# A decoder layer with a state-space branch: the order of the state-space batches' parts

## The chip, the cores and the metric

The kernel runs on one core of one Trainium2 chip. The metric is device time in microseconds (us) of one execution, as the median of several. The engines are TensorE (PE in the profile; its weight loads are PEld), VectorE (DVE), ScalarE (ACT), GpSimd (POOL) and SyncE (SP, which here only issues DMAs). Each engine takes its instructions from its own queue in a fixed order.

## The reference

One layer over 1024 tokens of width 1024, all in float32:

```
proj = rms_norm(h, pre_norm_g) @ w_in
u_ssm, z_ssm, q, k, v, z_attn = split(proj)
# state-space branch: 32 groups of 16 channels, each with a 64-wide complex state
bu = einsum('blgp,gnp->blgn', u, b_bar)
states = associative_scan(s[t] = lam_bar * s[t-1] + bu[t])
y = einsum('blgn,gpn->blgp', states, c).real + d * u
g = gelu(y)
ssm_out = g * sigmoid(g @ w_glu + b_glu) * silu(z_ssm)
# attention branch: window of 128 tokens, ALiBi, a sink logit per head
attn_out = swa(q, k, v, sinks) * silu(z_attn)
mixed = concat(ssm_out, attn_out) @ w_out
h = h + rms_norm(mixed, post_norm_g)
h = h + sigmoid(h @ pl_w_gate + pl_b_gate) * (p @ pl_w_proj)
```

## The kernel before

**Matrix products.** A projection is computed to full precision as three products of rounded parts, hi*hi, hi*lo and lo*hi (`products`, L115 to L126). Weights come in from DRAM to `w_st` (L98), ScalarE rounds them to `w_hi` (L92), and VectorE makes the rest `w_lo` (L93). A projection of 128 output columns over all tokens is 48 matmuls of 128x512.

**The state-space branch** is cut into eight batches of four groups. 1024 steps are cut into 128 chunks of 8. Within a chunk the recurrence is written as matrices, over the chunks a scan of 128 steps runs. For each batch:

- `into_states` (L513) loads the inputs `U` and the coefficients `coef` by SyncE; makes the matrix `mt` by three VectorE products (L335, the helper `tt`); transposes it on TensorE (L536) and copies it to `m` on ScalarE (L537); multiplies `U` by `m` (L541) and copies the result `w` (L543); makes the copy `w2` of `w` with its two halves of partitions exchanged, by two DMAs issued from ScalarE (L591, L592); makes the short-range matrix `t7` (L547, VectorE), writes it to DRAM four times (L558) and reads it back as the Toeplitz matrix `tz` (L560); and makes the output matrix `qt` by three VectorE products.
- `phases` (L568) makes `co` and `si`, the turning factors, by six VectorE products.
- `scan` (L595) turns `w` by `w2*si`, `w*co` and their sum, runs the scan on VectorE (L602) into `s`, and makes the exchanged copy `s2` by two DMAs from SyncE.
- `outputs` (L607) turns `s` back (`s2*si`, `s*co`, their difference), multiplies by `tz` and `qt` on TensorE (L615, L617), applies gelu on ScalarE (L619) into `y`, and stores `y` to DRAM (L622).

Most of these tiles come from pools of one or two buffers each, shared by a tag: `w` and `s` share the tag "w"; `w2`, `s2` and `y` the tag "sw"; the temporary products the tag "ta"; all three tags have two buffers. A tile that is asked for later takes the buffer of the tile asked for two before it, when that one's last reader is done.

**Order.** The program is written once, in order, and a planner lays out every engine's queue from it: each instruction's place is its place in the text, blocks under `high_priority(offset=20)` count as 20 instructions earlier, and the planner takes what by its own reckoning of times is ready first. What it has laid out is fixed when the kernel runs. `issue_after(x)` puts the instructions of its block behind instruction x on x's engine.

The main loop (L693) runs, for each batch c, at high priority: `scan(c)`, `phases(c+1)`, `outputs(c)`, `into_states(c+1)`. Then come one or two of eleven projections (v, four of q, four of z_attn, two of z_ssm).

**What follows the batches.** The last two z_ssm projections (`SsmGate`, L843) need nothing of the state space. The gate products of the state-space branch (`Glu`, L880; matmuls L903) read `y_all`, the outputs of all eight batches reloaded from DRAM by eight DMAs (L923), which SyncE issues behind the last exchange of `s`. The attention units (`Unit`, L744: scores L764 and L765, transposes L803, values L821) run beside the gate products and the first half of the output projection; their ScalarE parts are issued behind the gelu of the last batch (L983). Their queries are split to `bq_hi` and `bq_lo` (L733) in buffers that the state-space batches used before (tags "mt", "tz", "m" and "sw"). Then come the rest of the output projection, the norm, and the last gate product.

Of the kernel before, what the change touches and what calls it, by code (L numbers as in the profile page):

```python
# [20 lines left out]
P = 128  # L21
# [32 lines left out]
def layer_kernel(  # L54
# [6 lines left out]
    with ExitStack() as top:  # L61
# [272 lines left out]
        def tt(o, a, b, op):  # L334
            V.tensor_tensor(out=o, in0=a, in1=b, op=op)  # L335
# [144 lines left out]
        def big(name, tag):  # L480
            return t2([P, WID], F32, name, tag)
# [16 lines left out]
        def of_in(L, c):  # L498
            return L[:, c * GB : c * GB + GB, :].unsqueeze(2).broadcast_to([P, GB, PC, CH])
# [4 lines left out]
        def view_in(t):  # L504
            return t.rearrange("p (g q k) -> p g q k", k=CH, q=PC)

        def view_out(t):
            return t.rearrange("p (g k q) -> p g k q", k=CH, q=PC)
# [1 line left out]
        def ev(t):  # L510
            return t.rearrange("p (g a b) -> p g a b", a=8, b=16)

        def into_states(b):  # L513

            c = b["c"]
            gs = slice(c * GB, (c + 1) * GB)
            U = b["U"] = t2([P, GB, NC], F32, "U", "u")
            nc.sync.dma_start(out=U, in_=u_dr[c // 2][(c % 2) * 64 : (c % 2) * 64 + 64].rearrange("(g q) j c -> (q j) g c", q=PC))
            coef = b["coef"] = t2([P, GB, 4, PC], F32, "coef", "coef")
            with tc.issue_after(loaded.ins):  # L520
                nc.sync.dma_start(out=coef, in_=bc[:, gs])

            t1, mt = big("t1", "ta"), big("mt", "mt")
            def per_in(n):
                return coef[:, :, n, :].unsqueeze(3).broadcast_to([P, GB, PC, CH])

            def per_out(n):
                return coef[:, :, n, :].unsqueeze(2).broadcast_to([P, GB, CH, PC])

            tt(view_in(t1), of_in(LB_re_, c), per_in(0), ALU.mult)  # L530
            tt(view_in(mt), of_in(LB_im_, c), per_in(1), ALU.mult)
            tt(mt, t1, mt, ALU.subtract)
            m = big("m", "m")
            ps = bank("tab")
            for g in range(GB):
                PE.transpose(ps[:, g * P : (g + 1) * P], mt[:, g * P : (g + 1) * P], ident)  # L536
            S.copy(out=m, in_=ps)  # L537
            w = b["w"] = big("w", "w")
            ps = bank("w")
            for g in range(GB):  # L540
                PE.matmul(ps[:, g * NC : (g + 1) * NC], lhsT=m[:, g * P : (g + 1) * P], rhs=U[:, g, :],  # L541
                          start=True, stop=True)
            S.copy(out=w, in_=ps)  # L543
            b["w2"] = swapped(w, nc.scalar)
            ps = bank("tab")
            for g in range(GB):
                PE.matmul(ps[:, g * PC : (g + 1) * PC], lhsT=mt[:, g * P : (g + 1) * P],  # L547
                          rhs=coef[:, g, 2, :], start=True, stop=True)
            t7 = b["t7"] = t2([P, GB, PC], F32, "t7", "t7")
            tt(t7, last.unsqueeze(1).broadcast_to([P, GB, PC]),  # L550
               ddt[:, gs].unsqueeze(2).broadcast_to([P, GB, PC]), ALU.mult)
            tt(t7, t7, ps[:, 0 : GB * PC].rearrange("p (g q) -> p g q", q=PC), ALU.add)


            n, o = 2 * CH * PC, t7_dr[c].offset
            tz = b["tz"] = big("tz", "tz")
            for g in range(GB):
                nc.sync.dma_start(out=bass.AP(tensor=t7_dr.tensor, offset=o + g * PC * n + n - PC, ap=[[n, PC], [-PC, CH], [1, PC]]), in_=t7[:, g, :])  # L558
            for g in range(GB):
                nc.sync.dma_start(out=tz[:, g * P : (g + 1) * P],  # L560
                                  in_=bass.AP(tensor=t7_dr.tensor, offset=o + g * PC * n + CH * PC, ap=[[n, PC], [-PC, CH], [1, P]]))
            a, qt = big("t2", "ta"), big("qt", "qt")
            tt(view_out(a), of_out(L_re, c), per_out(2), ALU.mult)
            tt(view_out(qt), of_out(L_im, c), per_out(3), ALU.mult)
            tt(qt, a, qt, ALU.add)
            b["qt"] = qt

        def phases(b):  # L568
            gs = slice(b["c"] * GB, (b["c"] + 1) * GB)
            co, si = b["co"], b["si"] = big("co", "co"), big("si", "si")  # L570

            def a_(t):
                return t[:, gs, :].unsqueeze(3).broadcast_to([P, GB, 8, 16])

            def b_(t):
                return t[:, gs, :].unsqueeze(2).broadcast_to([P, GB, 8, 16])

            a = big("t3", "ta")
            tt(ev(a), a_(e1[1]), b_(e0[1]), ALU.mult)
            tt(ev(co), a_(e1[0]), b_(e0[0]), ALU.mult)  # L580
            tt(co, co, a, ALU.subtract)
            a = big("t4", "ta")
            tt(ev(a), a_(e1[0]), b_(e0[1]), ALU.mult)
            tt(ev(si), a_(e1[1]), b_(e0[0]), ALU.mult)
            tt(si, si, a, ALU.add)

        swaps = []

# [5 lines left out]

        def scan(b):  # L595
            w, w2, co, si, c = (b[n] for n in ("w", "w2", "co", "si", "c"))
            tt(w2, w2, si, ALU.mult)
            tt(w, w, co, ALU.mult)
            tt(w, w, w2, ALU.add)
            s = b["s"] = big("s", "w")  # L600
            for g in range(GB):
                V.tensor_tensor_scan(out=s[:, g * NC : (g + 1) * NC],  # L602
                                     data0=r8[:, c * GB + g : c * GB + g + 1].broadcast_to([P, NC]),
                                     data1=w[:, g * NC : (g + 1) * NC], initial=0.0, op0=ALU.mult, op1=ALU.add)
            b["s2"] = swapped(s, nc.sync)

        def outputs(b):  # L607
            s, s2, co, si, c, U, tz, qt = (b[n] for n in ("s", "s2", "co", "si", "c", "U", "tz", "qt"))
            tt(s2, s2, si, ALU.mult)
            tt(s, s, co, ALU.mult)  # L610
            tt(s, s, s2, ALU.subtract)
            y = t2([P, GB, NC], F32, "y", "sw")
            ps = bank("y")
# [71 lines left out]
        batch = [dict(c=c) for c in range(G // GB)]  # L685
        k_copies = [partial(copy_k, kv, part) for kv in range(2) for part in (kk_hi, kk_lo)]
        with tc.high_priority(offset=AHEAD):
            into_states(batch[0])
            phases(batch[0])
        project_k()  # L690
# [1 line left out]
                 + [partial(project_z_ssm, m) for m in range(2)])  # L692
        for c, b in enumerate(batch):  # L693
            with tc.high_priority(offset=AHEAD):
                scan(b)
                if c + 1 < len(batch):
                    phases(batch[c + 1])
                outputs(b)
                if c + 1 < len(batch):
                    into_states(batch[c + 1])  # L700
            for f in tiles[len(tiles) * c // len(batch) : len(tiles) * (c + 1) // len(batch)]:
                f()
                if k_copies and c > 1:
                    with tc.issue_after(w_last[0].ins):
                        k_copies.pop()()
# [479 lines left out]
```

## Time and profile before

| | us |
|---|---|
| median of 3 runs | 532.2 |
| lowest and highest of them | 531.94, 533.16 |
| the profiled execution | 531.67 |
| its span, from the first to the last instruction | 529.9 |
| the first scan of a batch begins | 90.0 |
| the last scan of a batch ends | 235.85 |

The profile is of one execution. Its rows give for a group of instructions the line of the kernel, the engine, the operation, the output tile and the input tiles, the shapes, and how many there were. In a row of the timeline the first number is the start and the second the duration, both in us from the start of the span; a row with x4 spans four instructions; the bracket at its end tells how long the engine was idle ahead of it, and on what it waited. Matmuls overlap, so the distance from one start to the next says more than a matmul's duration. ACTq and SPq rows are the issuing of DMAs. "Granted clock" is the share of full speed that TensorE's clock had.

### The profile page before, as it was taken

Reading aid. Unit: us, or ns where it says so; the run is one execution under the profiler, and the core shown is the slowest. Engines: PE = TensorE matmul, PEld = TensorE weight load, DVE = VectorE, ACT = ScalarE, POOL = GpSimd, SP = SyncE. Lnnn points to the kernel's source line nnn. Section 1 sums busy time; section 2 is a strip of 40 time slices with the busy share of each in tenths; the row PEclk is TensorE's granted clock in tenths of the full one; section 3 lists DMA queues with packets and bytes.
Section 4 is the critical chain, followed back from the end, with each engine's and each line's share of the span. In section 5 each row is a group of like instructions: output and inputs, shape, how many; then the busy total and the mean of one; then the engine's idle time right before and its main releaser. Section 6 shows DMA issues by size and latency. Waiting matters only on the chain.

```text
span 529.9 us, 7312 instructions
## 1 busy us (share of the span) xinstructions
PE 516.9 (98%) x2477; PEld 409.0 (77%) x2477; DVE 374.6 (71%) x865; ACT 211.7 (40%) x442; POOL 27.5 (5%) x69
## 2 busy tenths in 40 slices
PE   7999999999999999997899999999999999999996
PEld 6888888888888888884355766777788788888886
DVE  4879999879789979654878566555756659846232
ACT  5875121311222222124655655566734343333221
POOL 1000000000000000204020211100000000000000
PEclk9999999999999999999799999999999999999999
DMA  7972633445343344547755222101112155125112
GB/s 265 375 239 61 232 86 98 126 109 156 106 127 103 95 137 114 168 140 216 244 176 169 81 71 49 51 21 41 61 58 80 43 176 154 46 81 177 61 40 79
DMA packets 47092, 65.04 MB, mean 123 GB/s; under 512 B 10064, under 2 KB 25936, under 8 KB 47056
## 3 DMA queue, kind: packets, MB, share of 16 engines
q1 hardware_dynamic: 43664, 58.09, 34.5%
q0 software_dynamic: 1536, 4.20, 3.3%
q10 hardware_dynamic: 1856, 2.31, 1.7%
q8 instruction: 19, 0.31, 0.3%
q14 instruction: 17, 0.14, 0.1%
HBM read 44.12 MB, written 11.01 MB: 104 GB/s over the span
## 4 chain that ended last, share of the span: by engine, by line
PE 51%; DMA 2%; DVE 1%; SPq 0%; issue 0%; ACT 0%; ACTq 0%
PE ps_mm L126 9%; PE ps_mm L124 9%; PE ps_mm L122 9%; PE ps_mm L903 5%; PE ps_tab L122 3%; PE ps_tab L124 3%; PE ps_tab L126 3%; PE ps_w L821 2%; PE ps_y L821 2%; PE ps_tab L764 1%; PE ps_tab L765 1%; DMA y_all<-y_dr 1%; PE ps_w L803 1%; PE ps_y L803 1%; DMA y_dr<-y 1%
## 5 line engine op out<-in xcount | busy, mean ns | idle before, releaser
L122 PE MATMUL ps_mm<-x_hi,w_hi 128*128 128x512 f32 x272 | 86.2, 394 | 1.1 <-ACT x_hi L190 1.1
L126 PE MATMUL ps_mm<-x_hi,w_lo 128*128 128x512 f32 x272 | 86.9, 394 | 0.0
L124 PE MATMUL ps_mm<-x_lo,w_hi 128*128 128x512 f32 x272 | 85.7, 393 | 0.7 <-DVE x_lo L191 0.6
L92 ACT ACTIVATE w_hi<-w_st 128x512 fp32r<-128x512 f32 (+1 forms) x63 | 39.1, 621 | 100.9 <-PE ps_mm L124 68.9
L122 PEld LDWEIGHTS ps_mm<-x_hi,w_hi 128*128 128x128 f32 x272 | 50.9, 189 | 11.5 <-ACT x_hi L190 1.5
L124 PEld LDWEIGHTS ps_mm<-x_lo,w_hi 128*128 128x128 f32 x272 | 50.7, 188 | 11.6 <-DVE x_lo L191 1.5
L93 DVE TENSOR_TENSOR w_lo<-w_st,w_hi 128x512 fp32r<-128x512 f32 (+1 forms) x63 | 42.3, 671 | 24.3 <-ACT w_hi L92 24.3
L126 PEld LDWEIGHTS ps_mm<-x_hi,w_lo 128*128 128x128 f32 x272 | 50.7, 188 | 10.0
L903 PE MATMUL ps_mm<-y_all,w_glu 128*128 128x512 f32 x64 | 31.4, 637 | 3.5 <-DMA y_all<-y_dr 3.4
L122 PE MATMUL ps_mm<-h_hi,w_hi 128*128 128x512 f32 (+1 forms) x96 | 30.8, 380 | 0.0
L124 PE MATMUL ps_mm<-h_lo,w_hi 128*128 128x512 f32 (+1 forms) x96 | 30.8, 380 | 0.0
L126 PE MATMUL ps_mm<-h_hi,w_lo 128*128 128x512 f32 (+1 forms) x96 | 30.7, 380 | 0.0
L788 ACT ACTIVATE sc<-sc,mx 128x129 f32<-128x129 f32 x64 | 25.1, 395 | 12.7 <-DVE mx L781 12.5
L903 PEld LDWEIGHTS ps_mm<-y_all,w_glu 128*128 128x128 f32 x64 | 12.3, 203 | 17.7 <-issue 12.5
L1082 DVE SCALAR_TENSOR_TENSOR o_t<-o_t,pls 128x512 f32<-128x512 f32 (+1 forms) x17 | 10.8, 657 | 19.7 <-ACT o_t L1081 19.7
L335 DVE TENSOR_TENSOR sw<-sw,si 128x512 f32<-128x512 f32 x16 | 11.0, 686 | 16.5 <-DMA sw<-s 9.0
L122 PE MATMUL ps_mm<-m_hi,w_hi 128*128 128x512 f32 x64 | 22.1, 405 | 0.0
L126 PE MATMUL ps_mm<-m_hi,w_lo 128*128 128x512 f32 x64 | 21.8, 398 | 0.0
L124 PE MATMUL ps_mm<-m_lo,w_hi 128*128 128x512 f32 x64 | 21.7, 403 | 0.0
L122 PEld LDWEIGHTS ps_mm<-h_hi,w_hi 128*128 128x128 f32 x96 | 18.0, 188 | 3.5
L124 PEld LDWEIGHTS ps_mm<-h_lo,w_hi 128*128 128x128 f32 x96 | 18.1, 188 | 3.5
L126 PEld LDWEIGHTS ps_mm<-h_hi,w_lo 128*128 128x128 f32 x96 | 18.0, 188 | 3.4
(281 smaller groups left out, 1036.7 us busy)
## 6 DMA issues: line engine op xcount, KB each, us to landing
w_st<-in_w_in SPq DMA_DIRECT2D x30, 256.0 KB
w_st<-in_w_out SPq DMA_DIRECT2D x16, 256.0 KB
w_st<-in_w_gate SPq DMA_DIRECT2D x16, 256.0 KB
x<-in_xS SPq DMA_DIRECT2D x8, 512.0 KB
out_T<-o_t SPq DMA_DIRECT2D x15, 256.0 KB
x_sq<-in_xT SPq DMA_DIRECT2D x4, 512.0 KB
x_st<-in_x SPq DMA_DIRECT2D x4, 512.0 KB
x_sq<-in_x SPq DMA_DIRECT2D x4, 512.0 KB
```

What stands on the lines that cost most here:

```text
L92: S.activation(hi, t, AF.Copy)
L93: V.tensor_tensor(out=lo, in0=t, in1=hi.bitcast(F32), op=ALU.subtract)
L122: yield PE.matmul(o, lhsT=wh, rhs=ah(ka, h), start=f, stop=False)
L124: yield PE.matmul(o, lhsT=wh, rhs=al(ka, h), start=False, stop=False)
L126: yield PE.matmul(o, lhsT=wl, rhs=ah(ka, h), start=False, stop=l)
L335: V.tensor_tensor(out=o, in0=a, in1=b, op=op)
L764: PE.matmul(o, lhsT=l, rhs=kk_hi[:, kv, k0 : k0 + wk], start=True, stop=False)
L788: S.activation(self.sc[:, m, :], self.sc[:, m, :], AF.Exp, bias=self.mx[:, m : m + 1], scale=-1.0, accum_out=self.sm[:, m : m + 1])
L803: PE.transpose(pt[:, m * P : (m + 1) * P], self.sc[:, m, 0:P], ident)
L821: PE.matmul(pv[64 * kv : 64 * kv + 64], lhsT=v[:, cols], rhs=p[:, 2 * kv : 2 * kv + 2, :], start=n == 0, stop=n == len(parts) - 1)
L903: PE.matmul(self.ps, lhsT=self.w[:, k, :], rhs=glu_in["y"][:, self.hf, k, :], start=k == 0, stop=k == 3)
L1082: V.scalar_tensor_tensor(out=t, in0=t, scalar=1.0, in1=pls[2 * m + h][:, a : a + n], op0=ALU.add, op1=ALU.mult)
```

## The change

`into_states` is cut in two. The new `inputs` loads `U` and `coef`, makes `mt`, transposes it and copies it to `m`; `into_states` begins with the product by `m`. The main loop now runs, for each batch c: `inputs(c+1)`, `scan(c)`, `into_states(c+1)`, `phases(c+1)`, `outputs(c)`. In `scan` and in `outputs` the product with the tile itself comes before the product with its exchanged copy. And in `outputs` both products are issued behind the last product of `qt` (`made`) and the last of `si` (`turned`) of the following batch; the last batch has none to follow.

```diff
-        def into_states(b):
+        def inputs(b):
 
             c = b["c"]
             gs = slice(c * GB, (c + 1) * GB)
...
             t1, mt = big("t1", "ta"), big("mt", "mt")
...
+            b["mt"] = mt
+            tt(view_in(t1), of_in(LB_re_, c), per_in(b, 0), ALU.mult)
+            tt(view_in(mt), of_in(LB_im_, c), per_in(b, 1), ALU.mult)
             tt(mt, t1, mt, ALU.subtract)
-            m = big("m", "m")
+            m = b["m"] = big("m", "m")
             ps = bank("tab")
             for g in range(GB):
                 PE.transpose(ps[:, g * P : (g + 1) * P], mt[:, g * P : (g + 1) * P], ident)
             S.copy(out=m, in_=ps)
+
+        def into_states(b):
+
+            c, U, coef, m, mt = (b[n] for n in ("c", "U", "coef", "m", "mt"))
+            gs = slice(c * GB, (c + 1) * GB)
             w = b["w"] = big("w", "w")
             ps = bank("w")
...
-            tt(qt, a, qt, ALU.add)
+            b["made"] = V.tensor_tensor(out=qt, in0=a, in1=qt, op=ALU.add)
             b["qt"] = qt
...
-            tt(si, si, a, ALU.add)
+            b["turned"] = V.tensor_tensor(out=si, in0=si, in1=a, op=ALU.add)
...
         def scan(b):
             w, w2, co, si, c = (b[n] for n in ("w", "w2", "co", "si", "c"))
+            tt(w, w, co, ALU.mult)
             tt(w2, w2, si, ALU.mult)
-            tt(w, w, co, ALU.mult)
             tt(w, w, w2, ALU.add)
...
-        def outputs(b):
+        def outputs(b, behind):
             s, s2, co, si, c, U, tz, qt = (b[n] for n in ("s", "s2", "co", "si", "c", "U", "tz", "qt"))
-            tt(s2, s2, si, ALU.mult)
-            tt(s, s, co, ALU.mult)
+
+            with ExitStack() as after:
+                for i in behind:
+                    after.enter_context(tc.issue_after(i.ins))
+                tt(s, s, co, ALU.mult)
+                tt(s2, s2, si, ALU.mult)
             tt(s, s, s2, ALU.subtract)
...
         with tc.high_priority(offset=AHEAD):
+            inputs(batch[0])
             into_states(batch[0])
             phases(batch[0])
...
             with tc.high_priority(offset=AHEAD):
+                following = batch[c + 1] if c + 1 < len(batch) else None
+                if following:
+                    inputs(following)
                 scan(b)
-                if c + 1 < len(batch):
-                    phases(batch[c + 1])
-                outputs(b)
-                if c + 1 < len(batch):
-                    into_states(batch[c + 1])
+                if following:
+                    into_states(following)
+                    phases(following)
+                outputs(b, [following["made"], following["turned"]] if following else [])
```

More of the change, by code (lines that the diff above doesn't have):

```diff
@@ L511, in ev, with per_in, per_out @@
             return t.rearrange("p (g a b) -> p g a b", a=8, b=16)
-        def into_states(b):
+        def per_in(b, n):
+            return b["coef"][:, :, n, :].unsqueeze(3).broadcast_to([P, GB, PC, CH])
+        def per_out(b, n):
+            return b["coef"][:, :, n, :].unsqueeze(2).broadcast_to([P, GB, CH, PC])
+        def inputs(b):
             c = b["c"]
@@ L523, in into_states @@
             t1, mt = big("t1", "ta"), big("mt", "mt")
[L524 to L531, printed above, removed]
+            b["mt"] = mt
+            tt(view_in(t1), of_in(LB_re_, c), per_in(b, 0), ALU.mult)
+            tt(view_in(mt), of_in(LB_im_, c), per_in(b, 1), ALU.mult)
             tt(mt, t1, mt, ALU.subtract)
-            m = big("m", "m")
+            m = b["m"] = big("m", "m")
             ps = bank("tab")
@@ L562, in into_states @@
             a, qt = big("t2", "ta"), big("qt", "qt")
-            tt(view_out(a), of_out(L_re, c), per_out(2), ALU.mult)
-            tt(view_out(qt), of_out(L_im, c), per_out(3), ALU.mult)
-            tt(qt, a, qt, ALU.add)
+            tt(view_out(a), of_out(L_re, c), per_out(b, 2), ALU.mult)
+            tt(view_out(qt), of_out(L_im, c), per_out(b, 3), ALU.mult)
+            b["made"] = V.tensor_tensor(out=qt, in0=a, in1=qt, op=ALU.add)
             b["qt"] = qt
```

## The prediction

> **What bounds the kernel now.** I read the page first, then the busy times by stretch, then TensorE's own instructions where a stretch falls short, then the chain of waits that leads into that place. The page's first lines:
>
> ```profile
> span 529.9 us, 7312 instructions
> ...
> PE 516.9 (98%) x2477; PEld 409.0 (77%) x2477; DVE 374.6 (71%) x865; ACT 211.7 (40%) x442; POOL 27.5 (5%) x69
> ```
>
> TensorE (PE) is busy in 516.9 of 529.9 us. Only 13 us of the span are open to any reordering, unless matmuls that count as busy are themselves slow. So the question is where the missing time lies. Busy time by stretch (columns: PE, weight load, VectorE, ScalarE, GpSimd, granted clock, DMA share, GB/s):
>
> ```profile
> 60.00:220.00 160.00, 160.00 (x839) 136.59 (x838) 145.03 (x277) 38.29 (x57) 2.52 (x4) 1.00 0.43 119
> 220.00:239.10 19.10, 19.10 (x97) 15.87 (x95) 7.47 (x13) 2.81 (x4) 2.04 (x5) 1.00 0.58 175
> 239.10:262.50 23.40, 18.52 (x63) 9.77 (x62) 14.68 (x46) 12.48 (x35) 7.21 (x13) 0.85 0.80 236
> 262.50:380.00 117.50, 117.50 (x562) 79.09 (x561) 78.70 (x251) 74.56 (x219) 13.69 (x31) 1.00 0.28 83
> ```
>
> From 60 to 239 us, where the state-space batches run beside the projections, TensorE never lacks work. VectorE (DVE) is busy in 145 of the first 160 us, so it nearly is a second bound. From 239.1 to 262.5 TensorE stands still for 23.40 - 18.52 = 4.88 us, and the granted clock falls to a mean of 0.85. That is the seam between the last state-space batch and what needs all batches. TensorE's instructions in it:
>
> ```profile
> 253.53 3.78 PE L903 MATMUL ps_mm<-y_all,w_glu 128*128 128x512 f32 x4 [2.42 <-DMA y_all<-y_dr]
> 257.11 1.06 PE L803 MATMUL ps_w<-ident,sc 128*128 128x128 f32 x4
> 257.96 4.07 PE L903 MATMUL ps_mm<-y_all,w_glu 128*128 128x512 f32 x8
> 261.95 0.65 PE L821 MATMUL ps_w<-p,v_f 128*64 128x256 f32 x4
> 262.54 7.13 PE L903 MATMUL ps_mm<-y_all,w_glu 128*128 128x512 f32 x16
> 269.11 0.68 PE L764 MATMUL ps_tab<-kk,bq 128*128 128x256 f32 x1
> ```
>
> The gate products (L903) wait for y_all, the reloaded outputs of all batches. At full clock 16 of them take 269.11 - 262.54 = 6.57 us, 0.41 each. The four at 253.53 take 257.11 - 253.53 = 3.58 instead of 1.64 us (1.94 lost), the eight at 257.96 take 3.99 instead of 3.28 (0.71 lost). The four transposes between them take 0.85; I count half of it as lost, by the ratio of their neighbours: 0.42. With the 4.88 of standing still the seam costs 4.88 + 1.94 + 0.71 + 0.42 = 7.9 us. What ends it, from the chain that ended last:
>
> ```profile
> 244.01 0.58 ACT y L619
> ...
> 246.57 3.40 DMA y_dr<-y
> ...
> 250.11 3.37 DMA y_all<-y_dr
> ```
>
> The last batch's gelu at 244.01, its store to DRAM, and the reload that lands at 253.48. Attention's exponentials are queued behind the same gelu. So the seam shrinks exactly as far as the last batch's chain comes earlier against TensorE's other work. By how far is it late through waits that the change touches? VectorE's waits from 60 to 262 us (total, times, longest):
>
> ```profile
> DVE sw L335 <- DMA sw<-s: 9.0, 4, 3.1
> DVE z_half L866 <- PE ps_mm L126: 6.5, 1, 6.5
> DVE sw L335 <- DMA t_dr<-t: 5.6, 2, 3.0
> ```
>
> The first and third are the same place: the product with the exchanged halves of s stands at the head of VectorE's queue before the exchange has landed (the second name is another transfer that ended about then). Together 14.6 us. The last batch's chain, on VectorE and then on ScalarE:
>
> ```profile
> 219.62 0.68 DVE L335 TENSOR_TENSOR s<-s,sw 128x512 f32<-128x512 f32 x1
> 226.85 2.03 DVE L866 SCALAR_TENSOR_TENSOR z_half<-ps_mm,preb 128x512 f32<-128x512 f32 x2 [6.55 <-PE ps_mm L126]
> 230.81 0.69 DVE L335 TENSOR_TENSOR sw<-sw,si 128x512 f32<-128x512 f32 x1 [1.93 <-DMA sw<-w]
> ...
> 234.48 1.37 DVE L602 TENSOR_TENSOR_SCAN s<-r,w 128x128 f32<-128x128 f32 x4
> 238.96 0.69 DVE L335 TENSOR_TENSOR sw<-sw,si 128x512 f32<-128x512 f32 x1 [3.12 <-DMA sw<-s]
> ```
>
> ```profile
> 217.31 0.56 ACT L543 COPY w<-ps_w 128x512 f32<-128x512 f32 x1
> 225.47 0.63 ACT L92 ACTIVATE bq_hi<-q_f 128x512 fp32r<-128x512 f32 x1 [7.60 <-PE ps_y L615]
> 225.98 0.47 ACTq L591 DMA_DIRECT2D sw<-w  x1
> ```
>
> w of batch 7 is copied by 217.87, but its exchange is issued at 225.98, 8.1 us later: its buffer is free only once batch 6's s is made (219.62 + 0.68 = 220.30), and on ScalarE's queue it stands behind a query split that waits 7.60 us for batch 6's output matmuls. VectorE meanwhile has nothing of the batch to do.
>
> **The change, part by part.** *Inputs ahead of the scan.* Three products (3 x 0.68 = 2.0 us of VectorE), two loads, four transposes and a ScalarE copy of batch c+1 now come before scan(c). None is new. On VectorE the 2.0 us lie where it waits for an exchange anyway; if that cover were gone, each scan would be 2.0 us later. On SyncE the two loads pass ahead of the exchange of s; at the 0.47 us of an issue (the row at 225.98) that is 0.9 us if they are ready, and a held queue if the load of U has to wait for the output matmuls of c-1, which are queued on TensorE long before scan(c).
>
> *into_states(c+1) ahead of outputs(c).* The order in which the tiles of the tag "sw" (two buffers) are asked for changes from s2(c), y(c), w2(c+1) to s2(c), w2(c+1), y(c). The exchange of w(c+1) then takes the buffer of y(c-1), stored a batch ago, not that of s2(c). For batch 7 that frees the 225.98 issue to move to between 217.87 (w copied) and 220.30 at the latest on its data: 5.7 to 8.1 us, if the query split no longer stands before it, and nothing if it does. On SyncE, four stores of t7 and four loads of tz (8 x 0.47 = 3.8 us of issue) move ahead of the y stores of c. Nobody but the next buffer and the final reload waits for those stores, and after batch 7 there is no following batch, so the last stores are not delayed. On ScalarE, the copy of w(c+1) and two exchange issues come ahead of gelu(c), which has a batch of time.
>
> *s·co first, both behind "made" and "turned".* Between the scan and the two products VectorE now has at least the three qt and six phase operations, 9 x 0.68 = 6.1 us, against waits of 3.12 us at most. So the wait for s2 goes in batches 0 to 6. The last batch has nothing queued and keeps its 3.12. Gone: 14.6 - 3.1 = 11.5 us of VectorE time before scan(7). It costs nothing in added work: the nine operations were due anyway, and now fill the hole. What becomes late is s(c), below as a rival. *w·co first in scan* lets 0.68 us run before the exchange of w is needed, worth at most 0.68 of the 1.93 at 230.81.
>
> *Sum.* The chain of batch 7 can come earlier by 11.5 us (waits) plus 0 to 8.1 us (exchange of w): 11.5 to 19.6, less what the planner fills with other work. TensorE's own other work lasts until 253.53 - 2.42 = 251.11, so 2.4 us earlier ends the largest wait, and about 5 ends all of the standing still, since the sum of it is 4.88. Half of the smaller bound is enough. Nothing of TensorE's work is added or removed, and past 262.5 us it is the bound, so what is saved in the seam reaches the end. Between 0 and 7.9 I take 7.0: near the upper end because the lead is twice what is needed, 0.9 short because y_all still takes 3.37 us to load behind whatever precedes it. The profiled execution is 531.67 us, so 531.67 - 7.0 = 524.7; the median of the three runs, 532.2, is 0.5 above it: **525.2 us**.
>
> [...]
>
> **The rivals.** *Held outputs stall TensorE (slower).* With nine operations, and perhaps two tile operations of 0.68, in front, s(c) is ready 6.1 to 7.5 us after the scan, where now a wait of 3.0 us stands; that is 3.1 to 4.5 us later. What slack has TensorE's fixed order?
>
> ```profile
> 119.25 0.68 DVE L335 TENSOR_TENSOR s<-s,sw 128x512 f32<-128x512 f32 x1
> ```
>
> ```profile
> 120.16 0.38 PE L617 MATMUL ps_y<-s,qt 128*128 128x127 f32 x2
> ...
> 223.93 0.38 PE L617 MATMUL ps_y<-s,qt 128*128 128x127 f32 x2
> ```
>
> In batch 1 the output matmul follows s by 120.16 - 119.93 = 0.2 us, in batch 6 by 223.93 - 220.30 = 3.6; mean 1.9. If the planner leaves L617 where it is in TensorE's order, TensorE stands 3.1 - 1.9 = 1.2 to 2.6 us in each of seven batches, 8 to 18 us, against 7.0 saved: +1 to +11, middle 538. It decides from a mean delay of 1.9 + 1.0 = 2.9 us. For it: the slack of 0.2. Against it: the order is planned anew, with the edges known, so L617 should move as well. [...] No wait of L617 in this trace shows it.
>
> *Attention gives it back (no change).* Attention starts earlier, and its matmuls fall otherwise among TensorE's work. Rows of both kinds:
>
> ```profile
> 294.40 0.65 PE L821 MATMUL ps_y<-p,v_f 128*64 128x256 f32 x2
> 294.98 0.33 PE L803 MATMUL ps_w<-ident,sc 128*128 128x128 f32 x1
> 295.24 0.65 PE L821 MATMUL ps_y<-p,v_f 128*64 128x256 f32 x2
> ...
> 304.88 0.65 PE L821 MATMUL ps_w<-p,v_f 128*64 128x256 f32 x4
> 305.37 0.60 PE L821 MATMUL ps_w<-p_own,v_step 128*64 128x256 f32 x4
> ```
>
> Two value matmuls and one transpose in turn take 0.84 us; four value matmuls in a row 0.49, two 0.25. So each turn costs at least 0.84 - 0.25 - 0.33 = 0.26, and four turns a unit 1.0 us. Seven of the sixteen units falling worse would return 7 us: 532. It may as well help by some units: three give -3 us.
>
> *The lead does not reach the seam (half).* If the exchange of batch 7 stays behind the query split, or y_all has to wait for a buffer of the projection inputs, half of the seam stays: 532.2 - 3.9 = 528.3.
>
> **How the numbers follow.** A difference under 0.2% (1.1 us) is no change that a measurement of this kernel can tell. The forecast has 0.60: three independent waits point the same way and half of them suffice. Half of the seam 0.12, no change 0.11, slower 0.17. Faster is 0.60 + 0.12 = 0.72. The range goes from 532.2 - 7.9 - 3 = 521.3, the whole seam and three units falling better, to 534.0, which takes in the no-change case and the lower end of the stalling one; left out are most of that rival and a little below. The likeliest case alone spans 522 to 528.
>
> **What would show it.** Right: no wait for the exchange of s before scan(7), the exchange of w(7) issued within 3 us of its copy, gelu(7) at or before 238, clock 1.00 between 235 and 265, and TensorE's busy time in the seam full. Wrong: TensorE waits for s at L617 in batches 0 to 6 (the stalling rival), L903 still waiting over 2 us for y_all (half), or a longer stretch from the last gate product to the end of attention (given back).

## The result, and the profile after

| | before | after |
|---|---|---|
| median of the runs side by side, us | 532.07 (4 runs, 531.22 to 533.16) | 523.71 (4 runs, 523.43 to 525.7) |
| ratio, 95% interval | | 0.985 [0.9819, 0.988] |
| the profiled execution, us | 531.67 | 525.7 |
| its span, us | 529.9 | 523.8 |
| exchange of w(7) issued, us | 225.98 | 191.32 |
| gelu of the last batch, us | 244.01 | 214.17 |

The kernel is 8.4 us faster; 7.0 were forecast. The profiled execution is the slowest of the four: its first 20 us hold 61 matmuls against 71 before, as the clock was at 0.50 from 13.84 to 17.26 us, where it was at 1.00 before; by estimate that is 1.7 of the 1.7 to 2.3 us by which it lies above the others. The page, and the same four stretches as before the change:

```profile
span 523.8 us, 7300 instructions
PE 515.3 (98%) x2477; PEld 409.4 (78%) x2477; DVE 373.0 (71%) x865; ACT 212.6 (41%) x442; POOL 26.2 (5%) x69
```

```profile
60.00:220.00 160.00, 160.00 (x853) 136.86 (x852) 149.33 (x292) 41.21 (x63) 6.18 (x14) 1.00 0.49 135
220.00:239.10 19.10, 19.10 (x93) 16.01 (x93) 9.47 (x21) 6.40 (x15) 1.35 (x2) 1.00 0.33 113
239.10:262.50 23.40, 23.40 (x89) 13.59 (x88) 14.80 (x49) 13.44 (x41) 6.09 (x12) 1.00 0.95 268
262.50:380.00 117.50, 117.50 (x561) 80.58 (x561) 75.70 (x233) 70.55 (x201) 10.45 (x25) 1.00 0.26 72
```

The third row is the seam: TensorE was busy 18.52 us at a clock of 0.85, and now is busy all 23.40 at 1.00. All of TensorE's waits in the whole span:

```profile
PE ps_mm L122 <- ACT x_hi L190: 1.6, 1, 1.6
PE ps_y L222 <- POOL ident masks.py:199: 1.6, 1, 1.6
PE ps_mm L124 <- DVE x_lo L191: 0.6, 1, 0.6
PE ps_w L139 <- DVE sumsq L1060: 0.2, 1, 0.2
PE ps_y L163 <- DVE postr L156: 0.2, 1, 0.2
```

The first three belong to the start of the kernel and the last two to its final norm. The gate products (now L916) and the output matmuls (now L627) appear nowhere. The last batch's chain, first ScalarE, then VectorE (scan now L608, gelu L629, exchange L597):

```profile
190.70 0.59 ACT L549 COPY w<-ps_w 128x512 f32<-128x512 f32 x1 [2.08 <-PE ps_w L547]
191.32 0.47 ACTq L597 DMA_DIRECT2D sw<-w  x1
...
214.17 0.58 ACT L629 ACTIVATE y<-ps_y 128x512 f32<-128x512 f32 x1
```

```profile
130.15 0.69 DVE L335 TENSOR_TENSOR s<-s,co 128x512 f32<-128x512 f32 x1 [0.64 <-DMA sw<-s]
...
199.74 1.37 DVE L608 TENSOR_TENSOR_SCAN s<-r,w 128x128 f32<-128x128 f32 x4
...
206.16 0.69 DVE L335 TENSOR_TENSOR s<-s,co 128x512 f32<-128x512 f32 x1 [2.57 <-DMA sw<-s]
```

The exchange of w is issued right behind its copy (it was 8.1 us behind it), and of the waits for an exchanged s two are left, 0.64 us in an earlier batch and 2.57 us in the last. Batches follow each other faster: from the first scan to the last, seven steps took (234.48 - 90.0) / 7 = 20.6 us each and now take (199.74 - 92.1) / 7 = 15.4. The gelu is 29.84 us earlier, where 11.5 to 19.6 were forecast.

### The profile page after: what moved, and what is told of

Same layout as the page of the kernel before. It is cut to its first block, busy times and chain, and to the rows that moved or that the text cites. A ratio compares the mean times of both kernels' runs of the same rounds, so it can differ in the third digit from the quotient of the medians.

```text
span 523.8 us, 7300 instructions
## 1 busy us (share of the span) xinstructions
PE 515.3 (98%) x2477; PEld 409.4 (78%) x2477; DVE 373.0 (71%) x865; ACT 212.6 (41%) x442; POOL 26.2 (5%) x69
## 4 chain that ended last, share of the span: by engine, by line
PE 95%; DMA 2%; DVE 1%; ACT 0%; issue 0%; SPq 0%
PE ps_mm L122 21%; PE ps_mm L124 21%; PE ps_mm L126 21%; PE ps_mm L916 5%; PE ps_tab L122 4%; PE ps_tab L124 4%; PE ps_tab L126 4%; PE ps_w L834 2%; PE ps_y L834 2%; PE ps_tab L777 2%; PE ps_tab L778 2%; PE ps_y L625 1%; PE ps_y L627 1%; PE ps_w L547 1%; DMA x_st<-in_xT 1%; PE ps_tab L553 1%
## 5 line engine op out<-in xcount | busy, mean ns | idle before, releaser
L122 PE MATMUL ps_mm<-x_hi,w_hi 128*128 128x512 f32 x272 | 89.2, 401 | 1.6 <-ACT x_hi L190 1.6
L124 PE MATMUL ps_mm<-x_lo,w_hi 128*128 128x512 f32 x272 | 87.4, 399 | 0.6 <-DVE x_lo L191 0.6
L916 PE MATMUL ps_mm<-y_all,w_glu 128*128 128x512 f32 x64 | 28.7, 595 | 0.0
L916 PEld LDWEIGHTS ps_mm<-y_all,w_glu 128*128 128x128 f32 x64 | 11.7, 190 | 13.3 <-issue 12.4
L786 DVE COPY_PREDICATED ps_tab<-own,ps_tab 128x256 f32<-128x256 int32 x28 | 11.9, 425 | 11.1 <-PE ps_tab L778 11.1
```

The lines of the kernel that those rows point to most:

```text
L122: yield PE.matmul(o, lhsT=wh, rhs=ah(ka, h), start=f, stop=False)
L124: yield PE.matmul(o, lhsT=wh, rhs=al(ka, h), start=False, stop=False)
L786: V.copy_predicated(out=ps[:, :, 0:P], mask=own.unsqueeze(1).broadcast_to([P, 2, P]), data=ps[:, :, P : 2 * P])
L916: PE.matmul(self.ps, lhsT=self.w[:, k, :], rhs=glu_in["y"][:, self.hf, k, :], start=k == 0, stop=k == 3)
```

## The experiments

The theory after the result: the time lies in the seam alone, the seam closes as far as gelu(7) comes earlier, and what brings it earlier is the order of the batch's parts. Rivals: the hold behind `made` and `turned` does it; the buffer of w2 does it; the time comes from attention. The first group of kernels does parts of the change alone, the second sets how late the last batch is. All ratios are to the kernel before, run beside them on the same chip; it took 531.28 to 531.43 us there, against 532.07 beside the change, so between rows of different groups the ratios compare better than the times. The last column counts the matmuls that TensorE starts before the first output matmul of batch 7 that reads s; it is 1187 in the kernel before and 1051 in the changed one.

| kernel | us | ratio [interval] | exchange of w(7) | gelu(7) | step from scan to scan | matmuls ahead of the last outputs |
|---|---|---|---|---|---|---|
| after, without the hold | 523.12 | 0.9848 [0.9827, 0.9869] | 188.87 | 211.72 | 15.4 | 1051 |
| before, with the hold and the order of the products | 532.29 | 1.0024 [1.0011, 1.0037] | 226.38 | 244.83 | 20.7 | 1187 |
| before, inputs ahead of the scan | 531.84 | 1.002 [1.0, 1.004] | 226.37 | 245.20 | 20.8 | 1187 |
| before, buffer of w2 asked for early | 531.09 | 1.0002 [0.999, 1.0015] | 225.41 | 243.44 | 20.7 | 1187 |
| before, into_states ahead of outputs | 526.35 | 0.9905 [0.9875, 0.9936] | 202.96 | 224.44 | 17.6 | 1099 |
| before, the same for the last batch alone | 533.24 | 1.0037 [1.0019, 1.0055] | 217.58 | 240.31 | 19.5 | 1182 |

**The hold taken out of the changed kernel.**

```diff
-                outputs(b, [following["made"], following["turned"]] if following else [])
+                outputs(b, [])
```

> The changed kernel without the hold: the products with s and its exchanged copy are no longer issued behind made and turned; the new order of the parts stays. Theory (any lead over about 5 us closes the seam, more is not needed): VectorE waits for the exchange of s come back in part (5 to 12 us in all), the last gelu lies between 215 and 232, and the time stays within 1 us of the changed kernel, 523 to 525. Rival (the hold is what carries the gain): the last gelu is later than 238 and the time is 528 to 532.

Nothing came back: 523.12 us, as fast as the whole change, with VectorE waiting 2.58 us for the exchanged s in one place, the last batch, where 5 to 12 us were expected. The gelu, at 211.72, came even earlier than expected. So the hold is not what filled the holes.

**The hold alone.** The kernel before with both products behind `turned`, and s·co and w·co first. `made` can't be had here, since into_states, which makes `qt`, still comes behind outputs.

```diff
-                outputs(b)
+                outputs(b, [batch[c + 1]["turned"]] if c + 1 < len(batch) else [])
```

> The kernel before with the hold alone: in scan and outputs the product with the tile itself comes first, and both products of outputs are issued behind the last product of si of the following batch; into_states stays whole and behind outputs. Theory: the waits for the exchanged s go (14.6 us fall to under 5), the last gelu comes 8 to 15 us before 244.0 and the seam closes: 524 to 527. Rival (the order of the parts is what frees the chain, since the exchange of w still waits for s): the gelu moves by under 4 us, and the time is 529 to 533.

532.29 us, a little slower than before. VectorE's longest waits from 60 to 262 us:

```profile
DVE s L335 <- DMA sw<-s: 14.7, 6, 3.4
DVE z_half L869 <- PE ps_mm L126: 6.0, 1, 6.0
```

Before the change there were 14.6 us of the same wait. The planner laid the phases ahead of the scan, so being behind `turned` keeps nothing between the scan and the product. My expectation missed; the rival hit.

**into_states ahead of outputs, for every batch.** Nothing held, inputs not split off, products in their old order.

```diff
                 if c + 1 < len(batch):
                     phases(batch[c + 1])
-                outputs(b)
                 if c + 1 < len(batch):
                     into_states(batch[c + 1])
+                outputs(b)
```

> The kernel before with one move: into_states(c+1) ahead of outputs(c) in every batch; inputs not split off, nothing held, products in the old order. Theory (the exchange of w(c+1) no longer waits in line behind outputs(c), batch after batch, and that alone shortens the step from scan to scan): scans about 17 us apart against 20.6 before and 15.4 in the changed kernel, gelu(7) at 222 to 228 us, no wait of TensorE for y_all, the end of attention covered, 523 to 525.5 us. Rival (the inputs must be split off ahead of the scan as well, since the transposes and the copy to m otherwise stand between two exchanges): gelu(7) after 235, scans 19 us or more apart, 528 to 532 us.

gelu(7) came at 224.44, as expected; 526.35 us is 5.0 of the 8.4 and a little above the expected range, and a wait for y_all was left that was not expected. TensorE's waits that the whole change does not have:

```profile
PE ps_mm L903 <- DMA y_all<-y_dr: 1.1, 1, 1.1
PE ps_tab L536 <- DVE mt L335: 0.7, 1, 0.7
PE ps_mm L122 <- ACT w_hi L92: 0.7, 1, 0.7
PE ps_y L617 <- DVE s L335: 0.5, 1, 0.5
```

They sum to 3.0 us, about the 526.35 - 523.71 = 2.6 that are missing. The second is what the early inputs remove: the transposes wait for `mt`. The last is the place of the stalling rival, TensorE waiting for a late s, at 0.5 us instead of 8 to 18.

**The inputs alone.** `inputs` is split off as in the change; in the loop:

```diff
+                if c + 1 < len(batch):
+                    inputs(batch[c + 1])
                 scan(b)
```

> The kernel before with the inputs of batch c+1 split off ahead of scan(c), and nothing else: into_states(c+1) stays behind outputs(c). The last output matmuls keep their place in TensorE's order (219.0 us of its matmul work, as before; 200.1 with into_states moved alone, 189.2 in the changed kernel). Theory (the place of w and of the outputs in the queues is what counts; the early inputs are worth something only once into_states stands ahead of outputs): exchange of w(7) after 222 us, gelu(7) at 240 to 245, 530 to 533 us. Rival (the two moves add up, and the inputs alone are worth the 3 us by which the moved into_states falls short of the whole change): gelu(7) at 234 to 239, 527 to 529.5 us.

531.84 us: nothing gained, and the chain is where it was. One wait of the prediction's list showed: the loads of U, moved ahead on SyncE, were late, and TensorE stood for them.

```profile
PE ps_w L548 <- DMA U<-u_dr: 2.1, 2, 1.1
```

So the early inputs are worth about 3 us only behind the other move; the two do not add up from the kernel before, since into_states behind outputs keeps the step at 20.8 us.

**The buffer alone.** All queues are in the order they had; only the tile for the exchange of w(c+1) is asked for behind scan(c), which gives it the buffer that it has in the changed kernel.

```diff
-            b["w2"] = swapped(w, nc.scalar)
+            b["w2"] = swapped(w, nc.scalar, b.get("room"))
...
                 scan(b)
+                if c + 1 < len(batch):
+                    batch[c + 1]["room"] = big("sw", "sw")
```

> The kernel before with every queue in the order it had; only the buffer of w2(c+1) is asked for right behind scan(c), ahead of y(c), so that the exchange of w(c+1) takes the buffer it has in the changed kernel and no longer that of s2(c). Theory (the place in the queues sets the lead, ScalarE's above all, where the exchange of w(7) stands behind the query split): exchange of w(7) still at 225 to 227, gelu(7) at 243 to 245, 531 to 532.5 us. Rival (the buffer is what held it): exchange at 218 to 221, gelu(7) at 236 to 239, 526 to 529 us.

No difference (1.0002). ScalarE's queue around the exchange of w(7):

```profile
216.69 0.57 ACT L543 COPY w<-ps_w 128x512 f32<-128x512 f32 x1
224.89 0.63 ACT L92 ACTIVATE bq_hi<-q_f 128x512 fp32r<-128x512 f32 x1 [7.63 <-PE ps_y L615]
225.41 0.47 ACTq L591 DMA_DIRECT2D sw<-w  x1
```

The buffer is free and the exchange still goes out 8.1 us behind the copy, because the query split stands before it and waits for batch 6's output matmuls on TensorE. Of the prediction's two reasons for the 8.1 us the second is the one that acts. As TensorE's order is the old one too, and TensorE has no free time before 239 us, the gelu could hardly move here; whether the buffer would hold the exchange once the queue is clear was not tried.

**into_states ahead of outputs(6) only.**

```diff
+                if c + 2 == len(batch):
+                    into_states(batch[c + 1])
                 outputs(b)
-                if c + 1 < len(batch):
+                if c + 2 < len(batch):
                     into_states(batch[c + 1])
```

> The kernel before with one change: for the last batch alone, into_states comes ahead of the outputs of the batch before it. The waits for the exchanged s in the earlier batches stay. Theory (5 us of lead close the seam): the exchange of w of batch 7 is issued within 3 us of its copy instead of 8.1, the last gelu comes 5 to 8 us before 244.0, TensorE's standing still in the seam falls from 4.9 to under 1.5 us, and the kernel takes 525 to 527.5 us. Rival (the lead comes from the VectorE waits of all batches, and the last exchange hardly matters): the gelu moves by under 3 us and the time stays at 530 to 532.5.

533.24 us: a miss. The exchange of w(7) went out right behind its copy and the scan of batch 7 came 8.7 us earlier, but gelu(7) only 3.7, since the last output matmuls kept nearly their place in TensorE's order (1182 matmuls ahead, against 1187). What the seam gained was given back behind it. TensorE by stretch, in the seam and at the end of attention:

```profile
249.80:253.00 3.20, 3.20 (x7) 1.63 (x6) 1.21 (x1) 1.06 (x2) 0.00 (x0) 0.50 1.00 249
372.40:375.80 3.40, 1.68 (x13) 0.80 (x11) 3.04 (x6) 3.40 (x7) 0.00 (x0) 1.00 0.42 131
375.90:379.30 3.40, 2.94 (x8) 1.98 (x7) 3.40 (x7) 2.84 (x6) 0.00 (x0) 0.51 0.00 0
```

The seam holds 4.02 us of standing still from 230 to 290 (before: 4.88), still with a stretch at half clock, the first row. The other two rows are new: the last attention unit's parts come late, TensorE stands, and then runs a further 3.4 us at half clock. Before, it was busy in all of 290 to 400 us.

The second group sets the lateness of the last batch.

**The gate products without the late batches.** The kernel before; the last quarter of `y_all`, batches 6 and 7, is loaded from the stored outputs of batches 4 and 5, so this kernel leaves out that the gate products depend on the last two batches.

```diff
-                    glu_in["last"] = nc.sync.dma_start(out=y[:, hf, c, :].rearrange("p (i c) -> p i c", i=HC), in_=y_dr[c][:, HC * hf : HC * hf + HC, :])
+                    glu_in["last"] = nc.sync.dma_start(out=y[:, hf, c, :].rearrange("p (i c) -> p i c", i=HC), in_=y_dr[min(c, 2)][:, HC * hf : HC * hf + HC, :])
```

> The kernel before, where the last quarter of y_all is reloaded from the third quarter's store instead of its own, so that the gate products no longer depend on the last two batches (that part of the data is therefore another one). Attention still stands behind the last gelu. Theory in which cold matmuls go with the waits as a whole (no idle window left): the 2.42 us wait and the 3.07 us of slow matmuls go, 526 to 527.5. Theory in which they go in proportion: half of them stay, 528 to 529. If attention's own start is the limit of the seam, hardly anything changes: 530.5 to 532.5.

524.47 us, 0.9873 [0.9854, 0.9893], with gelu(7) at 243.99 as before: 6.9 us come with this one dependence gone, attention's share, below, included. TensorE still stands in the seam, but is not slow there (the clock is the third column from the end):

```profile
230.00:290.00 60.00, 56.98 (x231) 34.90 (x229) 43.46 (x116) 30.71 (x84) 11.17 (x22) 1.00 0.68 198
```

It stands 3.02 us in the seam and 2.32 at the end of attention, in sum more than the 4.88 before; yet 524.47 lies below every expected range. The gain is the clock and, as the lines further down show, attention.

**The last batch made late again.** The changed kernel with n GpSimd copies, s to s2 and back, between the turned s and the output matmuls of the last batch.

```diff
+            for _ in range(0 if behind else n // 2):
+                Q.tensor_copy(out=s2, in_=s)
+                Q.tensor_copy(out=s, in_=s2)
```

> The changed kernel with 8 more GpSimd copies (s to s2 and back) ahead of the last batch's two products; the last batch's outputs then hold scan values that the copies pass through, and its chain ends later. Place of the last output matmuls in TensorE's order 16.5 us of work later. Theory (a lead of 5 to 7 us against 244 is enough for the seam, the rest of the 30 us is not used): gelu(7) about 231, no wait for y_all, 523.0 to 524.7 us. Rival (every microsecond of lead is worth something): gelu(7) about 231, 526 to 528 us.

> The same with 12 copies, the last output matmuls 24.7 us of TensorE's work later than in the changed kernel: gelu(7) about 239, 5 us ahead of the kernel before. Theory (5 us of lead is enough, as the prediction had it): 523.5 to 525.5 us, waits of TensorE for y_all below 1 us in sum. Rival (the store, the reload and the eight loads of y_all take longer than the prediction allowed, so that 10 us or more of lead are needed): 526 to 529 us with y_all waits of 2 us or more.

> The changed kernel, with 16 copies of s on GpSimd, one after another, put in the last batch alone between the turned s and the output matmuls (they leave s as it is). At an estimated 0.8 us each (GpSimd's 128x512 select took 0.77 us) they delay the last gelu by about 13 us, from 214 to about 227. Theory (only a gelu later than about 239 costs): no change against the changed kernel, within 0.8 us. Rival (every microsecond of lead counts, since attention starts with the gelu): 3 to 8 us slower than the changed kernel.

> As with 16 copies, but 32: the last gelu about 26 us later, at about 240, which is 4 us before where it lay in the kernel before. Theory: this is at the edge; TensorE's standing still around the gate products stays under 2 us and the time is 523.5 to 526. Rival: 6 to 10 us slower than the changed kernel, 530 or more.

> As with 16 copies, but 48: the last gelu about 38 us later, at about 252, 8 us behind where it lay in the kernel before. Theory: the seam opens again and wider than before, with the clock halved in it: 533 to 541 us. If the time stays under 527, the seam was not what cost the kernel before its 8 us.

| copies | gelu(7) | us | ratio [interval] | TensorE still, 230 to 290 | clock there | value matmuls, busy |
|---|---|---|---|---|---|---|
| 0 (after) | 214.17 | 523.71 | 0.985 [0.9819, 0.988] | 0 | 1.00 | 25.5 |
| 8 | 228.97 | 522.55 | 0.9843 [0.9826, 0.9859] | 0 | 1.00 | 25.5 |
| 12 | 235.72 | 525.75 | 0.9907 [0.9879, 0.9935] | 3.12 | 1.00 | 22.9 |
| 16 | 245.74 | 529.14 | 0.9956 [0.9942, 0.9971] | 7.38 | 0.91 | 22.1 |
| 32 | 246.22 | 531.07 | 0.9989 [0.9978, 1.0001] | 6.64 | 0.91 | 23.6 |
| 48 | 246.21 | 530.47 | 0.9986 [0.9973, 0.9999] | 6.97 | 0.91 | 23.6 |

With 16 copies or more the last batch was not as late as meant. The 16 copies were done by 218.2 us; the output matmuls stood behind other work in TensorE's fixed order until 243.7, where the planner had put them. So 32 and 48 give the same gelu as 16, and the three expectations fell. But the table reads well by the gelu: at 229 the whole gain is there, at 236 2.0 us of it are gone (3.2 against 8 copies, which ran beside them), at 246 it is 5.4 to 7.4. With 12 copies, between its two expected ranges, TensorE did not wait for y_all but for the next piece of the gate's weights:

```profile
PE ps_mm L919 <- DMA w_glu<-in_w_glu: 3.1, 1, 3.1
```

```profile
236.32 2.84 SPq L635 DMA_DIRECT2D y_dr<-y  x4
242.61 0.81 SPq L939 DMA_DIRECT2D y_all<-y_dr  x2
...
244.44 0.98 SPq L910 DMA_DIRECT2D w_glu<-in_w_glu  x2
```

```profile
243.50:252.10 8.60, 5.52 (x22) 2.93 (x20) 6.79 (x19) 4.83 (x15) 3.57 (x6) 1.00 0.99 261
```

The stores come at 236.32, the last loads of y_all at 242.61, the weights at 244.44: all in one queue, one behind the other. The weights landed at 252.10, 7.7 us after their issue, as the DMA engines were busy for 0.99 of the time from 243.5 on (the last column but one). In the changed kernel they landed no earlier, at 252.88, and nothing waits: there attention's matmuls stand among the gate products, and TensorE comes to the product that needs these weights at 253.74. With 12 copies it was there at 249.02.

**Attention's share.** The last column of the table is the sum of four rows, the kinds of value matmuls (busy time of each; 120 matmuls in every kernel). Here they are, first before, then after:

```profile
L821 PE MATMUL ps_w<-p_own,v_step 128*64 128x256 f32 x28 | 6.9, 392 | 0.0
L821 PE MATMUL ps_y<-p,v_f 128*64 128x256 f32 x32 | 6.5, 404 | 0.0
L821 PE MATMUL ps_w<-p,v_f 128*64 128x256 f32 x32 | 5.9, 405 | 0.0
L821 PE MATMUL ps_y<-p_own,v_step 128*64 128x256 f32 x28 | 5.6, 390 | 0.0
```

```profile
L834 PE MATMUL ps_w<-p_own,v_step 128*64 128x256 f32 x28 | 7.7, 397 | 0.0
L834 PE MATMUL ps_w<-p,v_f 128*64 128x256 f32 x32 | 7.1, 404 | 0.0
L834 PE MATMUL ps_y<-p_own,v_step 128*64 128x256 f32 x28 | 5.5, 383 | 0.0
L834 PE MATMUL ps_y<-p,v_f 128*64 128x256 f32 x32 | 5.2, 405 | 0.0
```

24.9 us before and 25.5 after: attention hardly gave or took. With 12 copies it is 22.9, with the reload of the third quarter 22.2. Fewer of them stand in short runs there: runs of just two value matmuls are 17 before, 18 after, 11 with 12 copies and 10 with the reload, and runs of eight 7, 7, 10 and 11. So the term of that rival is real, 2 to 3 us, and it flatters these kernels. At the value matmuls' time of the kernel before, 24.9, the reload would stand, by estimate, at 524.47 + 2.7 = 527.2, against 531.42 for the kernel before beside it: it gains 4.2 and not 6.9. By TensorE's whole busy time over the last 2300 matmuls, less half of what was busy at half clock (473.4 us before, 472.7 after the change, 469.2 here), it gains 2.7, about what the half clock cost. So the reload shows the clock's part of the seam, not that of the standing still, of which it has as much as before. And the later last batch costs, by the same estimate and each against the changed kernel, 525.75 + 2.6 - 523.71 = 4.6 us with 12 copies, 529.14 + 3.4 - 523.71 = 8.8 with 16, 531.07 + 1.9 - 523.71 = 9.3 with 32 and 530.47 + 1.9 - 523.71 = 8.7 with 48. The last three now agree with each other, and with the 8.4 us of the change.

## Why the prediction was right, point by point

**Where the time lies: right.** The seam was priced at 7.9 us, and the change gained 8.4. All 4.88 us of standing still are gone, and the gate products, before and after, are 2.7 us shorter:

```profile
L903 PE MATMUL ps_mm<-y_all,w_glu 128*128 128x512 f32 x64 | 31.4, 637 | 3.5 <-DMA y_all<-y_dr 3.4
```

```profile
L916 PE MATMUL ps_mm<-y_all,w_glu 128*128 128x512 f32 x64 | 28.7, 595 | 0.0
```

That is 7.6 of the 8.4. The kernels with a late last batch agree: the changed kernel with its chain late again (gelu at 246) lost 5.4 to 7.4 us, and 8.7 to 9.3 at equal time for attention's value matmuls.

**Why the chain came earlier: half wrong.** The step that failed is "Gone: 14.6 - 3.1 = 11.5 us of VectorE time before scan(7)", put down to the hold. The hold alone does nothing and the change without it loses nothing. In its place: with into_states(c+1) ahead of outputs(c), the exchange of w(c+1) and the outputs of c no longer wait one for the other, batch after batch. Before the change, the exchanges of w of batches 4 to 7 go out 10.6, 7.8, 11.2 and 8.1 us behind their copies. In ScalarE's queue they stand behind the gelu of the batch before, or for batch 7 behind a query split, which waits for output matmuls. For batch 6:

```profile
193.64 0.59 ACT L543 COPY w<-ps_w 128x512 f32<-128x512 f32 x1 [3.92 <-DVE s L602]
...
205.23 0.60 ACT L619 ACTIVATE y<-ps_y 128x512 f32<-128x512 f32 x1 [0.66 <-PE ps_y L617]
205.47 0.47 ACTq L591 DMA_DIRECT2D sw<-w  x1
```

The step from scan to scan shows the sum: 20.6 us, 17.6 with this move, 15.4 with the early inputs too, 20.8 with the early inputs without it. The exchange of w, 0 to 8.1 in the sum, was right at its upper end, by the queue and not by the buffer.

The prediction added up waits of VectorE and ScalarE, and TensorE does not wait for these at the end of the chain. In every kernel here s(7) is ready before its first output matmul starts, 0.95 us before the change, 3.92 after it and 25.5 with 16 copies; and before and after the change TensorE lacks no work from 60 to 239 us. So gelu(7) comes when TensorE has done what stands ahead of these matmuls in its fixed order. Over all kernels here it goes with their number: 1051 ahead, gelu(7) at 212 to 214; 1099, 224; 1124 (8 copies), 229; 1164 (12), 236; 1182, 240; 1187, 243 to 245; 1195 (16 and more), 246. The change acts through the order that the planner lays out. Which parts move it the variants show; how the planner reckons it they don't.

**The size of the lead: wrong, without harm.** 11.5 to 19.6 us "less what the planner fills with other work" had the wrong sign. VectorE's idle time between the first and the last scan fell from 23.4 to 1.0 us; that is 22 us. The other 14 of the 37 us by which the scans came together are work on projections that stood between the scans and now comes later. The largest of these rows, from the first to the last scan before the change, have no counterpart after:

```profile
L667 DVE SCALAR_TENSOR_TENSOR z_half<-ps_mm,preb 128x512 f32<-128x512 f32 x4 | 4.0, 1077 | 0.0
L672 DVE SCALAR_TENSOR_TENSOR z_tanh<-z_tanh,z_half 128x1024 f32<-128x1024 f32 x2 | 2.4, 1215 | 0.0
L866 DVE SCALAR_TENSOR_TENSOR z_half<-ps_mm,preb 128x512 f32<-128x512 f32 x2 | 2.0, 1094 | 6.5 <-PE ps_mm L126 6.5
```

The shorter chain did not draw in more work; it pushed work out behind itself. The planner's reasons for that are not settled by these runs.

**"About 5 ends all of the standing still": too small.** With gelu(7) at 235.72, 8.3 us of lead, no wait for y_all was left, but 3.12 us for the gate's weights, which landed no later than in the changed kernel but found TensorE without other work; with 15.0 us (228.97) nothing was left. With into_states moved alone, 19.6 us of lead, TensorE still waited 1.1 us for y_all. So no one number says how much lead is needed: it depends on what else the order holds for TensorE at that point. That the forecast held although both the lead and the need came out larger is in part luck: the errors were in the same direction. What bounds the loads now is not the batch: all eight of y_all are issued from 237.09 on, 23 us behind the gelu (from 236.80 with into_states moved alone), as the prediction's "half" rival named (a buffer of the projection inputs), but early enough for the first gate product at 245.15. That it is this buffer was not tried alone.

**Held outputs stall TensorE: refuted here.** No wait at L627. The planner moved the output matmuls with s; in the batch with the least room they still follow s by 133.63 - (132.70 + 0.68) = 0.25 us:

```profile
132.70 0.68 DVE L335 TENSOR_TENSOR s<-s,sw 128x512 f32<-128x512 f32 x1
```

```profile
133.63 0.38 PE L627 MATMUL ps_y<-s,qt 128*128 128x127 f32 x2
```

**The slow matmuls: by the whole, not in proportion.** Half-clock stretches, before the change:

```profile
248.70:252.00 3.30, 1.09 (x7) 0.67 (x6) 2.51 (x5) 2.78 (x10) 2.39 (x4) 1.00 0.79 195
252.10:258.60 6.50, 5.07 (x9) 2.60 (x10) 4.46 (x17) 2.72 (x4) 0.30 (x1) 0.50 0.86 287
```

The clock was 0.50 for 6.50 us, 5.07 of them busy: by estimate half of these, 2.5 us, lost, where the prediction's price of the seam has 1.94 + 0.71 + 0.42 = 3.07 by the spacing of rows. It went as a whole wherever the standing still from 230 to 290 us was cut to 3.12 us or less (the reload kernel, 3.02, and 12 copies, 3.12, both at 1.00). The "half" rival's 3.9 us let it go in proportion, as half of the whole 7.9; a step was the better shape here. It did not matter for the forecast, since no waits were left.

**The sum.** 7.0 was 1.4 short. I left 0.9 of the seam standing for the 3.37 us of the reload; nothing was left of it. The other 0.5 is within the spread of the runs (523.43 to 525.7).

## What to carry to other kernels

In a software pipeline, look for pairs of steps that wait for each other in every round through the queue of a third engine, and put the next round's producer ahead of this round's consumer; the step from round to round shows at once whether the series is broken. Where the engine that bounds the kernel never lacks work, ask how much of its work stands ahead of the last round's part: that sets when the round ends, and waits on other engines matter as far as they move this place. Ask how much earlier the last round must be for the seam behind it to close, store, reload and the work that covers them included, and count lead beyond that at nothing. A wait that seems cured by one line of a change may be cured by another: undo that line alone.

## What the runs showed of the hardware

In these traces' record of the granted clock, the time from one change to the next is a whole multiple of 3.413 us. From the first change on there are 72, 2 and 79 of them before the change (at 6.30, 252.06, 258.88 and 528.54 us), and 2, 1 and 148 after it (at 7.02, 13.84, 17.26 and 522.43 us). In the kernel with the last batch moved, one stretch at half clock begins at 249.56 us and the next at 375.85, 37 of them later. Where these edges lie against the program differs: the first stretch at half clock in the seam begins at 252.06 us before the change, and at 252.57 with the buffer alone.

With the edges known, TensorE's busy time in the 3.41 us ahead of a change can be read (the clock is the third column from the end). Three such windows before the change, the first ahead of half clock, the last ahead of the return to 1.00:

```profile
248.65:252.06 3.41, 1.14 (x8) 0.72 (x6) 2.57 (x5) 2.83 (x10) 2.44 (x5) 1.00 0.79 194
252.06:255.47 3.41, 1.94 (x3) 0.91 (x4) 2.26 (x7) 0.00 (x0) 0.00 (x0) 0.50 0.89 291
255.47:258.88 3.41, 3.41 (x9) 1.75 (x8) 2.52 (x10) 3.00 (x5) 0.58 (x1) 0.50 0.84 280
```

Two after the change, again the one ahead of half clock and the one at half clock:

```profile
10.43:13.84 3.41, 1.18 (x5) 0.35 (x3) 1.37 (x2) 2.30 (x2) 0.00 (x0) 1.00 1.02 394
13.84:17.26 3.42, 3.42 (x8) 2.77 (x9) 3.41 (x4) 2.81 (x5) 0.00 (x0) 0.50 1.03 413
```

And two at full clock, of the kernels with 12 copies and with the last batch moved; only the second was followed by half clock:

```profile
247.30:250.71 3.41, 1.72 (x13) 1.35 (x11) 2.98 (x7) 1.52 (x3) 2.01 (x2) 1.00 1.03 259
372.44:375.85 3.41, 1.69 (x12) 0.78 (x10) 3.05 (x6) 3.41 (x8) 0.00 (x0) 1.00 0.41 126
```

So half clock followed windows with 1.14, 1.18 and 1.69 us of busy time, and 1.18 ahead of 249.56 with the last batch moved; it did not follow the one with 1.72 (the ends of matmuls are modelled, so 1.69 and 1.72 can't be told apart). None of the four was idle, where the expectation for the reload has the clock go with an idle window. At half clock, another such window followed the one with 1.94 us of busy time, and full clock the two that were busy throughout. With 12 copies a wait of 3.12 us at one go left the clock at 1.00; an edge lay in it, with 1.69 us of the wait ahead of it and 1.43 behind.

How long TensorE stood still did not alone tell how much half clock came with it. The kernel with the buffer alone stood still 5.02 us from 230 to 290, before the change it was 4.88; the first had one window at half clock, 252.57 to 255.99, the second two, 252.06 to 258.88 (mean granted clock of the profiled executions: 0.997 and 0.992). From 13.84 to 17.26 us, with TensorE busy throughout in both, 8 matmuls are in the window at 0.50 after the change and 17 at 1.00 before it; by estimate, half of its length, such a window costs 1.7 us.
